# Retention of a two-layer diffusion trunk on one core: two passes over the heads, and latent projections in pairs by seven block products

## The chip, the cores and the metric

The kernel runs on one core of a Trainium2 chip. The metric is the device time of one execution in microseconds (us); a kernel's time is the median over its runs. The engines are PE (matmul), DVE (vector), ACT (scalar), POOL (GpSimd) and SP, which here only issues loads and stores.

## The reference, cut to what matters

The trunk has two layers over 512 latent tokens and 256 context tokens of width 1024; each layer has a mixer and a gated feed-forward part (FFN), with RMS norms, shift, scale and gate around each. The mixer of layer 1 is a bidirectional retention of 8 heads (keys 128 wide, values 256). Context tokens give no output there (`ctx_out` is false), only the state from which the latent scans start:

```python
q, k, v, g = jnp.split(h_lat @ w_in, splits, axis=-1)
q = apply_rope(q.reshape(B, T, H, dk), cos, sin)
k = apply_rope(k.reshape(B, T, H, dk) * dk ** -0.5, cos, sin)
kc, vc = jnp.split(h_ctx @ w_in[:, RET_QK_WIDTH:2 * RET_QK_WIDTH + RET_V_WIDTH], [RET_QK_WIDTH], axis=-1)
for d in range(2):
    lg = log_decay[d]
    s_ctx = retention_final_state(rev(kc), rev(vc), lg)
    outs_lat.append(rev(retention_chunked(rev(q), rev(k), rev(v), lg, s_ctx)))
o = outs_lat[0] + outs_lat[1]
on = ((o - mu) * lax.rsqrt(var + EPS)) * gn_g          # per head
y_lat = (jax.nn.silu(g) * on) @ w_out
```

The layer's conditioning (six vectors of 1024 from `silu(c) @ ada_w[i] + ada_b[i]`) is computed in twelve halves of 512.

## The kernel before, in words

Every fp32 operand of a matmul is split into two parts, hi and lo (`split`, L97): ACT copies it rounded (hi), DVE subtracts (lo). A product (`mm3`, L140) is three matmuls: hi by hi, hi by lo, lo by hi. A unit of weights (`unit`, L101) is 128x1024 numbers that SP's queue loads into a ring of three raw buffers and `split` turns into one of a few slots (`at_slot`, L124; `slot`, L128).

The retention (L1146 to L1488) comes after FFN 0. Its inputs stand in SBUF, turned and split: `hl`, the latent tokens (512 columns), and `hc`, the context tokens (256), built from the residual stream by `build_h` behind the finisher (L641) of FFN 0; `need(chunk)` (L470) builds what isn't built yet. One loop runs over the heads (L1385). Head 0 is special, as its tokens come only then. Each other head does in turn:

- k and then q of all latent tokens (`proj_t`, PSUM names `rk`, `rq`), 24 matmuls of 512 columns each, with the rotation on ACT, DVE and POOL (`rope`, L1192: `m1`, `sw`) and between them the transposes `rt` of the head before (`gated`, L1358), whose gated and normed output goes to two features `gt`
- the output product of head h-1 (`out_group`, L626) for h up to 5, added into y in SBUF by DVE (`yr<-wr,yr`)
- the transposes of k (`k_nat`, L1217), values for the context and the latent tokens (`nat`, L1269: PSUM name `rn`, 48 matmuls of 256 columns for two tiles of 128 tokens), scores (`score`: `rs`, `sd`), states of context and latent chunks (`states`, L1241: `stc`, `stl`), then the gates by `nat` again
- inside and across the chunks (`within`, `across`: `ro`, `rx`, sums in `of`), the context keys of the next head (`k_ctx`, L1203: `rkc`), and the norm (`norm`, L1330: `rbs`, `rmv`, `rrr`, `on`).

The outputs of heads 5 to 7 are summed at the end in PSUM (`part`, L1461), added to y and handed to the finisher. Beside all this, `bg` (L244) steps background jobs: six halves of conditioning (L1886) by `ada_half` (L257), which multiplies on DVE, eight operations 512 wide in each half (`acc<-ar,cs,acc`), and folds them with `ac` or `ag` matmuls. The hybrid layer's halves go another way (`ada_packed`, L333): eight matmuls `ad` with the weights as they come.

The order of work is the order in which the program is written: each engine takes its instructions in that order, and POOL's and SP's queues of transfers likewise. Buffers come free by the rings and slots of the pools.

The FFNs already multiply blocks. The right operand is cut into 2 x 2 blocks (`alloc_blocks` L501, `build_piece` L523), seven sums and single blocks of it are kept (`block_sums`, L559), seven of the weights are made for each piece, and seven products replace eight; their results meet in PSUM (several products onto one sum) or in SBUF. There POOL adds pieces of y to DRAM by accumulating transfers (`yd<-yp`).

Of the kernel before, what the change touches and what calls it, by code (L numbers as in the profile page):

```python
# [31 lines left out]
GF = 2  # L32
ND = 389
EARLY = 2
MLP_PIECES = (
    ((0, (4, 5), 0, False), (0, (0,), 256, True), (1, (1, 2), 0, False), (1, (3,), 256, True)),
    ((0, (0, 1), 0, True), (1, (2,), 0, False), (1, (3,), 128, True)),
)
# [30 lines left out]
class Trunk:  # L69
# [430 lines left out]

    def alloc_blocks(self, l):  # L501
# [8 lines left out]
    def staged(self, l, half, k, w):  # L510
# [3 lines left out]
        if self.sb is None:  # L514
            homes = ((self.bp, "y0"), (self.lp, "y4"), (self.lp, "y5"), (self.lp, "G1")), ((self.bp, "y0"), (self.bp, "y1"))
# [7 lines left out]
    def build_piece(self, l, half, toks, c0, last, xn, ab):  # L523
# [20 lines left out]
        if half:  # L544
# [5 lines left out]
        for m in range(4):  # L550
            src = self.staged(l, half, 2 * m, 2)
            if half and m < 2:
                self.split(self.b12[0][m], self.b12[1][m], src)
            else:
                b = self.blk[(11, 21)[m // 2] if not half else 22]
                ks = slice(2 * (m % 2), 2 * (m % 2) + 2)
                self.split(b[:, 0, ks, :], b[:, 1, ks, :], src)

    def block_sums(self, l):  # L559
# [17 lines left out]
        hb = self.bp.tile([P, 6144], F32R, name=f"hs{l}", tag="h1", bufs=1)  # L577
        for i, x in enumerate((2, 4)):
            self.blk["t", x] = hb[:, 8 * n * i : 8 * n * (i + 1)].rearrange("p (x k c) -> p x k c", x=2, k=4)
        self.rest = hb[:, 16 * n :]  # L580
# [60 lines left out]
    def finisher(self, gates, src, ab, name, xts, last=False, mlp=None):  # L641
# [4 lines left out]
        def fin(t, y, sums=None):  # L646
            if not done and not last:
                if mlp is None:
                    self.alloc_h(name)
                else:  # L650
# [10 lines left out]
            if not last:  # L661
                for b in self.pend:
                    b[0] -= 1
                if mlp is None:
                    for c, pair in ((2, (4, 5)), (0, (0, 1)), (1, (2, 3))):
                        if t == pair[1]:
                            self.pend.append([1, c, lambda c=c: self.build_h(c, done, ab, name)])
                else:
                    for half, toks, c0, end in MLP_PIECES[mlp]:
                        if t == toks[-1]:  # L670
                            go = lambda h=half, ts=toks, c0=c0, e=end: self.build_piece(mlp, h, ts, c0, e, done, ab)
                            self.pend.append([1, half, go])
# [473 lines left out]
    def retention(self, y, final):  # L1146
        S, V, T, G, a = self.S, self.V, self.T, self.G, self.a
        KS = float(np.float32(P) ** np.float32(-0.5))
        with ExitStack() as ctx:
            rp = self.phase(ctx, "retp", 3)  # L1150
            dist = rp.tile([P, 2 * ND], F16, name="dist", tag="dist")
            self.load(dist, a["dist"])
            cos = rp.tile([P, 512], F32, name="cos", tag="cos")
            self.load(cos, a["cos"])
            sin = rp.tile([P, 512], F32, name="sin", tag="sin")
            self.load(sin, a["sin"])
            dec = rp.tile([P, 16], F32, name="dec", tag="dec")
            self.load(dec, a["decay"].broadcast_to([P, 16]))
            gng = rp.tile([P, 16], F32, name="gng", tag="gng")
            self.load(gng, a["gn_col"])  # L1160
            w8 = lambda w: [x.rearrange("p (k c) -> p k c", k=4) for x in w]

            def home(name):
# [842 lines left out]
```

## Time and profile before

| what | value |
| --- | --- |
| median of 3 runs | 1862.83 us (1862.36 to 1866.6) |
| the profiled execution's own time | 1862.51 us |
| its span in the trace | 1860.7 us |
| PE busy | 96% |
| DVE, ACT, POOL busy | 71%, 54%, 17% |
| mean granted TensorE clock | 0.987 |

The profile is of one execution, and its span lies 1.8 us under that execution's own time. All operations are recorded by one helper and so carry one line number (L61, in the changed kernel L64); rows are told apart by the names of their tiles, with the buffer numbers left out. In a row, `x` is a count, `out<-in` the tiles, and a bracket the idle time ahead of the operation and what ended it. The context keys' first matmuls, `rkc`, come at 933.8 us, and those of the following heads at 992.8, 1063.4, 1130.5, 1196, 1262, 1328 and 1387; the first of them marks the retention's begin, the others the last part of the head before. The tail runs from 1452 to 1500, and FFN 1 begins inside it, about 1481.

### The profile page before, as it was taken

The numbers are of one execution on the slowest core, as the hardware profiler recorded it, in microseconds if no ns is written. First come the engines' busy times: TensorE is split into PE (matmuls) and PEld (weight loads), VectorE is DVE, ScalarE is ACT, GpSimd is POOL, SyncE is SP. The second block draws the span as 40 slices with busy tenths as digits, with TensorE's granted clock in tenths as the row PEclk, the third lists the DMA queues.
The fourth block names the chain that finished last, engine by engine and source line by source line (L and its number), as shares of the span: only waits on it lengthen the run. The fifth ranks groups of instructions, "written<-read, shape, count | busy, mean of one in ns | idle before, by whom it ended". The sixth has DMA issues, their size and how long they took to land. (4 is left out here: it accounts for less than half of the span.)

```text
span 1860.7 us, 28942 instructions
## 1 busy us (share of the span) xinstructions
PE 1783.2 (96%) x11104; PEld 1587.4 (85%) x11104; DVE 1319.3 (71%) x2235; ACT 1005.4 (54%) x1815; POOL 314.5 (17%) x451
## 2 busy tenths in 40 slices
PE   7999999999999999998999999999999899999998
PEld 4887777889989899998787988998999689889887
DVE  4543567579787787778876676666555798888887
ACT  4534567456565555555564433443444476666664
POOL 1111211100223222221121011001000201122221
PEclk9999999999999999999999999999999989999999
DMA  8433332324587777776642431332222335777772
GB/s 308 136 105 106 105 103 74 120 82 147 154 198 159 164 159 155 170 148 153 222 151 63 130 109 52 126 114 66 83 69 62 120 108 150 185 182 175 185 172 103
DMA packets 83627, 249.79 MB, mean 134 GB/s; under 512 B 10912, under 2 KB 12448, under 8 KB 83488
## 3 DMA queue, kind: packets, MB, share of 16 engines
q1 hardware_dynamic: 56960, 199.00, 32.7%
q0 software_dynamic: 25952, 48.83, 15.3%
q8 instruction: 87, 1.43, 0.3%
q14 instruction: 52, 0.43, 0.1%
q10 hardware_dynamic: 576, 0.11, 0.0%
HBM read 191.28 MB, written 39.85 MB: 124 GB/s over the span
## 5 line engine op out<-in xcount | busy, mean ns | idle before, releaser
L61 DVE SCALAR_TENSOR_TENSOR cv<-pre,cw,cv 128x769 f32<-128x769 f32 (+1 forms) x176 | 152.9, 881 | 6.5 <-ACT cv L61 5.9
L61 DVE SCALAR_TENSOR_TENSOR acc<-ar,cs,acc 128x512 f32<-128x512 f32 x160 | 118.2, 751 | 30.0 <-DMA ar<-in_adaw 19.0
L61 ACT ACTIVATE cv<-pre,cw 128x770 f32<-128x770 f32 (+1 forms) x88 | 81.0, 922 | 43.1 <-DVE pre L61 41.8
L61 POOL DMA_DIRECT2D yf<-yp x64 | 55.7, 871 | 264.9 <-ACT yp L61 229.2
L61 POOL DMA_DIRECT2D yd<-yp x54 | 46.1, 861 | 190.8 <-ACT yp L61 186.9
L61 ACT COPY yp<-wf 128x512 f32<-128x512 f32 x118 | 67.8, 576 | 17.4 <-PE wf L61 17.3
L61 ACT ACTIVATE pre<-px 128x256 f32<-128x256 f32 (+2 forms) x160 | 54.1, 365 | 39.2 <-PE px L61 38.8
L61 POOL DMA_DIRECT2D yd<-ypg x54 | 44.8, 852 | 153.9 <-ACT ypg L61 153.2
L61 POOL TENSOR_SCALAR rrr<-rmv 128x2 f32<-128x2 f32 x16 | 3.1, 194 | 349.7 <-DVE rmv L61 349.7
L61 ACT ACTIVATE g<-cv 128x770 fp32r<-128x770 f32 (+1 forms) x44 | 32.5, 738 | 34.5 <-DVE cv L61 34.2
L61 PE MATMUL px<-hs,wd 128*128 128x384 f32 x240 | 45.4, 337 | 0.4 <-DVE pre L61 0.4
L61 PEld LDWEIGHTS px<-hs,wd 128*128 128x128 f32 x240 | 42.3, 188 | 2.3 <-DVE pre L61 0.8
L61 ACT ACTIVATE cv<-cv 128x770 f32<-128x770 f32 (+1 forms) x44 | 32.7, 744 | 17.2 <-DVE cv L61 17.1
L61 DVE TENSOR_TENSOR g<-cv,g 128x770 fp32r<-128x770 f32 (+1 forms) x44 | 36.2, 822 | 6.7 <-ACT g L61 6.2
L61 ACT ACTIVATE pre<-py 128x384 f32<-128x384 f32 (+1 forms) x40 | 17.3, 434 | 41.8 <-DVE cv L61 24.4
L61 PEld LDWEIGHTS px<-hs 128*128 128x128 f32 x240 | 30.8, 190 | 10.2 <-DVE pre L61 9.1
L61 PE MATMUL px<-hs 128*128 128x256 f32 x240 | 32.5, 285 | 7.0 <-DVE pre L61 7.0
L61 DVE TENSOR_TENSOR pre<-pre,pz 128x256 f32<-128x256 f32 (+1 forms) x60 | 20.9, 371 | 23.5 <-PE pz L61 23.4
L61 DVE TENSOR_TENSOR cv<-cv 128x770 f32<-128x770 f32 (+1 forms) x44 | 36.2, 822 | 1.0
L61 POOL TENSOR_TENSOR tm<-slab,mask 128x256 f32<-128x256 f32 (+1 forms) x32 | 25.6, 832 | 65.7 <-DVE sst L61 65.5
L61 ACT ACTIVATE sc<-sc,sst 128x512 f32<-128x512 f32 x32 | 23.2, 726 | 23.9 <-DVE sc L61 21.6
L61 ACT COPY ypg<-wf 128x512 f32<-128x512 f32 x54 | 30.8, 577 | 8.0 <-PE wf L61 7.9
(2535 smaller groups left out, 6751.2 us busy)
## 6 DMA issues: line engine op xcount, KB each, us to landing
ar<-in_adaw SPq DMA_DIRECT2D x96, 512.0 KB, 4.2
yf<-yp POOLq DMA_DIRECT2D x64, 256.0 KB, 4.4
yd<-yp POOLq DMA_DIRECT2D x54, 256.0 KB, 5.2
yd<-ypg POOLq DMA_DIRECT2D x54, 256.0 KB, 4.7
fin<-xd SPq DMA_DIRECT2D x10, 512.0 KB, 5.6
xd<-xd SPq DMA_DIRECT2D x8, 512.0 KB, 2.6
xn<-in_x SPq DMA_DIRECT2D x6, 512.0 KB, 5.7
xb<-in_x SPq DMA_DIRECT2D x6, 512.0 KB, 3.9
```

The costliest lines, as they stand in the source:

```text
L61: r = f(*p, **k)
```

## The change

The retention takes its heads in two passes. The first does only the context: keys, values and the final states of all eight heads. The raw states go to DRAM (`rsd`). During it the latent tokens, which now are cut into blocks of 256 tokens by 512 features (`alloc_ret`, `build_piece`), are built, and their sums are made behind context heads 1 to 4 (`block_sums("r")`).

The second pass does the latent heads. k and q of a head are one pair: their weights are the two rows of a 2 x 2 block matrix, and `kq_product` makes them by seven products of 12 matmuls, 256 columns each, into three PSUM tiles X, Y, Z. Values and gates are the other pair (`vg_product`: seven products of 24 matmuls). The weights' sums are made in place in the raw buffers by `sums`: per pair three additions on POOL (`rwk`, `rwq` 512 wide, `rwa`, `rwb` 1024) and one on DVE, with seven splits for a value pair and six for a key pair. These run as generators that are stepped between the products (`in_kq`, `in_vg`). The context's state is loaded back (`cs`) and split.

The output of heads 0 to 4 is cut into eight pieces a head, woven between the products of the next one (`out_steps`, `o`): ACT copies the piece into one of two buffers (`ryp`), and a transfer on POOL's queue adds it to DRAM (`yr`); y is loaded at the end. Head h-1's pieces start behind the sixth product of head h's k and q. The norm writes in place (`of`), `gated` reads `g`. The six conditioning halves beside it go by `ada_packed`. The loads of the decay numbers and a part of `dist` move ahead of FFN 0, those of `cos`, `sin` and `gng` to the sixth context head.

```diff
+CTX_BG = 1
...
+    def alloc_ret(self):
+
+        self.bn = 256
+        self.hb = [self.bp.tile([P, 3, 2048], F32R, name=f"h{i}c", tag=f"h{i}", bufs=1) for i in range(2)]
+        self.hc = [x[:, 0].rearrange("p (k c) -> p k c", k=KD) for x in self.hb]
+        view = lambda i, r: self.hb[i][:, r].rearrange("p (x k c) -> p x k c", x=2, k=4)
+        self.blk = {11: view(0, 1), 21: view(0, 2), 22: view(1, 1), ("t", 2): view(1, 2)}
+        self.sa = self.bp.tile([P, KD, 256], F32, name="sar", tag="sa", bufs=1)
+        self.sb = None
...
+        if l == "r":
+            hb = self.bp.tile([P, 3, 1024], F32R, name="sar4", tag="sa", bufs=1)
+            self.blk["t", 4] = hb[:, 0:2].rearrange("p x (k c) -> p x k c", k=4)
+            self.rest = hb[:, 2]
...
+                            self.pend.append([9 if mlp == "r" else 1, half, go])
...
+            states_d = [self.dp.tile([P, 512], F32, name=f"rsd{h}", tag=f"rsd{h}") for h in range(8)]
+            yd = [self.dp.tile([P, D], F32, name=f"yr{t}", tag=f"yr{t}") for t in range(4)]
...
+            def ctx_states(h):
+                d = hd[h]
+                kd = d["kdc"]
+                pc = self.ps(f"stc{h}", "A", (P, 2, 256))
+                for i in range(2):
+                    for t in range(2):
+                        self.mm3(pc[:, i], [x[:, t, i] for x in kd], [x[:, t] for x in d["vc"]], t == 0, t == 1)
+                sc = self.t2k(f"sc{h}")
+                S.copy(sc, pc.rearrange("p i v -> p (i v)"))
+                self.load(states_d[h], sc)
...
+            def sums(a1, a2, b1, b2, put, both=None):
+
+                add = lambda o, x, y: G.tensor_tensor(out=o, in0=x, in1=y, op=ALU.add)
+                if both:
+                    put("a1", both)
+                else:
+                    put("a1", a1)
+                    yield
+                    put("a2", a2)
+                add(a1, a1, b1)
+                add(b1, b1, b2)
+                yield
+                put("s2", b1)
+                V.tensor_tensor(out=b1, in0=a1, in1=b2, op=ALU.add)
+                add(a2, a2, b1)
+                yield
+                put("q3", b1)
+                yield
+                put("q4", a2)
+                yield
+                put("s3", a1)
+                yield
+                put("b2", b2)
...
+            def prod_t(ps, w, b, kind):
+                for k in range(4):
+                    c = slice(k * P, (k + 1) * P)
+                    self.mm3(
+                        ps,
+                        [x[:, c] for x in w],
+                        [self.blk[b][:, x, k, :] for x in range(2)],
+                        k == 0 and kind != "onto",
+                        k == 3,
+                        kind == "onto",
...
+            def kq_product(h, after):
+
+                d = hd[h]
+                w = d["kq"]
+                pre = [rp.tile([P, 512], F32, name=f"{x}p{h}", tag=f"pre{i}") for i, x in enumerate("kq")]
+                X, Y = (self.ps(f"{x}kq{h}", "A", (P, 256)) for x in "XY")
+                Z = self.ps(f"Zkq{h}", "C", (P, 256))
+                C = [slice(0, 256), slice(256, 512)]
+                k = d["k"] = [kq_[:, 0, x] for x in range(2)]
+                q = d["q"] = [kq_[:, 1, x] for x in range(2)]
+                prod_t(X, w["a1"], 11, "only")
+                S.copy(pre[0][:, C[0]], X)
+                after(0)
+                prod_t(Z, w["a2"], 21, "only")
...
+                V.tensor_tensor(out=pre[0][:, C[0]], in0=pre[0][:, C[0]], in1=Z, op=ALU.add)
+                after(1)
+                prod_t(Y, w["s2"], ("t", 1), "only")
+                S.activation(pre[1][:, C[1]], Y, AF.Copy, scale=-1.0)
+                after(2)
+                prod_t(X, w["q3"], ("t", 2), "onto")
+                S.copy(pre[0][:, C[1]], X)
+                after(3)
+                prod_t(Y, w["q4"], 22, "onto")
+                V.tensor_tensor(out=pre[0][:, C[1]], in0=pre[0][:, C[1]], in1=Y, op=ALU.add)
+                after(4)
+                d["kl"] = pre[0]
+                one, two = rope(pre[0], k, KS, f"k{h}")
+                one()
+                prod_t(X, w["s3"], ("t", 3), "onto")
+                V.tensor_tensor(out=pre[1][:, C[1]], in0=pre[1][:, C[1]], in1=X, op=ALU.subtract)
+                after(5)
+                two()
+                prod_t(X, w["b2"], ("t", 4), "onto")
+                S.activation(pre[1][:, C[0]], X, AF.Copy, scale=-1.0)
+                one, d["q_two"] = rope(pre[1], q, 1.0, f"q{h}")
+                one()
+                after(6)
...
+            def vg_product(h, after, o):
+
+                d = hd[h]
+                w = d["vg"]
+                v = d["v"] = [rp.tile([P, 4, 256], F32R, name=f"rv{i}{h}", tag=f"rv{i}", bufs=1) for i in range(2)]
+                g = d["g"] = rp.tile([P, 4, 256], F32, name=f"rg{h}", tag="rg", bufs=1)
+                X, Y, Z = (self.ps(f"{x}vg{h}", "A", (P, 2, 256)) for x in "XYZ")
+                C = [slice(0, 2), slice(2, 4)]
+                prod_n(X, w["a1"], 11, "only")
+                d["q_two"]()
+                pre = rp.tile([P, 2, 256], F32, name=f"vp0{h}", tag="pre1", bufs=1)
+                S.copy(pre, X)
+                after(0)
+                k_nat(h)
+                prod_n(Z, w["a2"], 21, "only", o)
+                V.tensor_tensor(out=pre, in0=pre, in1=Z, op=ALU.add)
+                self.split(v[0][:, C[0]], v[1][:, C[0]], pre)
+                after(1)
...
+            def context(h):
+                d = hd[h]
+                d["sc"] = rp.tile([P, 2, 256], F32, name=f"cs{h}", tag="cs", bufs=1)
+                self.load(d["sc"].rearrange("p i v -> p (i v)"), states_d[h])
+                d["st"] = [rp.tile([P, 4, 256], F32R, name=f"st{i}{h}", tag=f"st{i}", bufs=1) for i in range(2)]
+                self.split(d["st"][0][:, 0:4:3], d["st"][1][:, 0:4:3], d["sc"])
...
+            def out_steps(h, feats, wo):
+                if not parts:
+                    t = rp.tile([P, 2, 512], F32, name="ryp", tag="yp")
+                    parts.extend(t[:, i] for i in range(2))
+
+                def piece(t, n):
+                    c, o = self.gcol(t), H[n]
+                    ps = self.ps(f"w{h}{t}{n}", "B")
+                    for f, (g, w) in enumerate(zip(feats, wo)):
+                        self.mm3(ps, [x[:, c] for x in g], [x[:, o] for x in w], f == 0, f == 1)
+                    parts.append(parts.pop(0))
+                    S.copy(parts[-1], ps)
+                    if h == 0:
+                        G.dma_start(yd[t][:, o], parts[-1])
+                    else:
+                        G.dma_start(yd[t][:, o], parts[-1], accum_op=ALU.add)
+
+                return [lambda t=t, n=n: piece(t, n) for t in range(4) for n in range(2)]
...
+            blocks = self.block_sums("r")
+            ctx_weights(0)
+            self.need(2)
+            kq = vg = None
+            for h in range(8):
+                ctx_keys(h)
+                if h == 1:
+                    self.need(1)
+                if h:
+                    ctx_states(h - 1)
+                ctx_values(h)
+                if h < 7:
+                    ctx_weights(h + 1)
+                else:
+                    kq = kq_weights(0)
+                    next(kq)
+                    next(kq)
+                if h == 0:
+                    self.need(0)
+                elif h < 5:
+                    next(blocks, None)
+                if h == 5:
+                    self.load(cos, a["cos"])
+                    self.load(sin, a["sin"])
+                    self.load(gng, a["gn_col"])
+                if h == 6:
+                    vg = vg_weights(0)
+                self.bg(CTX_BG)
...
+                def in_kq(n):
+                    if n == 0:
+                        o()
+                        if h in (0, 6, 7):
+                            step(vg)
+                    elif n == 1:
+                        o()
+                        if 0 < h < 6:
+                            wo.append(w_out(h - 1))
+                    elif n == 2:
...
+                    elif n == 5:
+                        if h:
+                            f.extend(gated(h - 1))
+                            if h < 6:
+                                out.extend(out_steps(h - 1, f, list(wo)))
+                            else:
+                                feats.extend(f)
...
+                def in_vg(n):
+                    nonlocal later
+                    if n == 0:
+                        step(vg)
+                        self.bg()
+                    elif n == 1:
+                        step(vg)
+                    elif n == 2:
+                        step(vg)
+                        context(h)
+                        self.bg()
+                        if h < 7:
+                            later = kq_weights(h + 1)
+                    elif n == 3:
+                        step(vg)
+                        score(h, 0)
+                    elif n == 4:
+                        self.bg()
+                    elif n == 5:
+                        score(h, 1)
+                        states(h)
+                        within(h, 0)
+                        step(later)
...
+                kq_product(h, in_kq)
+                vg_product(h, in_vg, o)
...
+                        self.load(y[t], yd[t])
...
-        self.jobs = [self.ada_half(1, h, 1, g3 if h < 6 else None) for h in range(4, 10)]
+        self.jobs = [self.ada_packed(1, h, 1, g3 if h < 6 else None) for h in range(4, 10)]
```

Where latent head 3 begins, POOL's order before has the last part of head 2's norm (`rrr`), head 3's decay matrix (`e`), the sine products of k and q, and the clearing and first row of a conditioning half:

```order
L61 TENSOR_SCALAR rrr2_10872<-rmv2_10871 128x2
L61 TENSOR_TENSOR rrr2_10872<-rrr2_10872,mhalf_102 128x2
L61 TENSOR_TENSOR e03_10947<-e03_10947,e13_10949 128x384
L61 TENSOR_TENSOR e03_10947<-e03_10947,ident_80 128x128
L61 TENSOR_TENSOR swk3_10932<-swk3_10932,sin_8821 128x512
L61 TENSOR_TENSOR swq3_10996<-swq3_10996,sin_8821 128x512
L61 MEMSET acc170_11019 128x512
L61 DMA acc170_11019<-in_adab_row 1x16x32
```

The same place of the changed kernel, between heads 3 and 4 (`yr` are the pieces of y in DRAM, `rwa` and `rwb` the raw weights of values and gates):

```order
L64 TENSOR_TENSOR e04_12528<-e04_12528,e14_12530 128x384
L64 TENSOR_TENSOR rrr3_12426<-rrr3_12426,mhalf_102 128x2
L64 TENSOR_TENSOR e04_12528<-e04_12528,ident_80 128x128
L64 DMA yr2_8799<-ryp_10688 128x512
L64 DMA yr3_8800<-ryp_10688 128x512 x2
L64 TENSOR_TENSOR rwa14r_12387<-rwa14r_12387,rwb14r_12391 128x1024
L64 TENSOR_TENSOR rwb14r_12391<-rwb14r_12391,rwb24r_12389 128x1024
L64 TENSOR_TENSOR swk4_12579<-swk4_12579,sin_8786 128x512
L64 TENSOR_TENSOR swq4_12629<-swq4_12629,sin_8786 128x512
L64 TENSOR_TENSOR rwa24r_12393<-rwa24r_12393,rwb14r_12391 128x1024
```

The pieces' transfers and two wide additions now stand ahead of the sine products on POOL, and a third one behind them; the clearing of `acc` is gone.

DVE's order before, from the rotation of head 3's k to that of its q (`gt` are head 2's features, `yr` here y in SBUF):

```order
L61 SCALAR_TENSOR_TENSOR m1k3_10931<-rk3_10904,cos_8819 128x512
L61 SCALAR_TENSOR_TENSOR gt12_10954<-rt20_10955,gng_8825,gt02_10953 128x512
L61 TENSOR_TENSOR m1k3_10931<-m1k3_10931,swk3_10932 128x512
L61 SCALAR_TENSOR_TENSOR gt12_10954<-rt21_10962,gng_8825,gt02_10953 128x512
L61 TENSOR_TENSOR rk13_10930<-m1k3_10931,rk03_10929 128x512
L61 SCALAR_TENSOR_TENSOR m1q3_10995<-rq3_10946,cos_8819 128x512
L61 TENSOR_TENSOR yr00_9661<-wr200_11038,yr00_9661 128x512
L61 TENSOR_TENSOR m1q3_10995<-m1q3_10995,swq3_10996 128x512
```

And now (`kp` and `qp` are k and q before the rotation, which meet the sums X, Y, Z; `rwo` and `rvg` are lo parts of split weights):

```order
L64 TENSOR_TENSOR kp3_11809<-kp3_11809,Zkq3_11813 128x256
L64 TENSOR_TENSOR rwo21l_11859<-rwo21r_11860,rwo21h_11858 128x1024
L64 TENSOR_TENSOR rvga13l_11915<-rwa13r_11745,rvga13h_11914 128x1024
L64 TENSOR_TENSOR kp3_11809<-kp3_11809,Ykq3_11812 128x256
L64 TENSOR_TENSOR rvga23l_11932<-rwa23r_11751,rvga23h_11931 128x1024
L64 TENSOR_TENSOR qp3_11810<-qp3_11810,Xkq3_11811 128x256
L64 SCALAR_TENSOR_TENSOR kp3_11809<-kp3_11809,cos_8785 128x512
L64 SCALAR_TENSOR_TENSOR gt12_11956<-rt20_11957,gng_8784,gt02_11955 128x512
L64 SCALAR_TENSOR_TENSOR gt12_11956<-rt21_11964,gng_8784,gt02_11955 128x512
L64 TENSOR_TENSOR kp3_11809<-kp3_11809,swk3_11937 128x512
L64 TENSOR_TENSOR rvgs23l_11993<-rwb13r_11749,rvgs23h_11992 128x1024
```

The additions into y are gone from DVE, and the meets of the products and four wide splits stand between the steps of the rotation.

More of the change, by code (lines that the diff above doesn't have):

```diff
@@ L543, in build_piece @@
             return
-        if half:
+        if half and l != "r":
             n = self.bn
@@ new lines, in prod_t, with prod_n @@
+            def prod_t(ps, w, b, kind):
+                for k in range(4):
+                    c = slice(k * P, (k + 1) * P)
+                    self.mm3(
+                        ps,
[4 more added lines that the diff above has]
+                        kind == "onto",
+                    )
+            def prod_n(ps, w, b, kind, between=lambda: None):
+                for i in range(2):
+                    if i:
+                        between()
+                    for k in range(4):
+                        c = slice(i * P, (i + 1) * P)
+                        self.mm3(
+                            ps[:, i],
+                            [self.blk[b][:, x, k, c] for x in range(2)],
+                            [x[:, k, :] for x in w],
+                            i == 0 and k == 0 and kind != "onto",
+                            k == 3,
+                            True,
+                        )
@@ new lines, in two @@
+                def two():
+                    V.tensor_tensor(out=x, in0=x, in1=sw, op=ALU.add)
+                    self.split(dst[0], dst[1], x)
+                return one, two
+            def kq_product(h, after):
[34 more added lines that the diff above has]
+                after(6)
@@ L1253, in states @@
+                for i in range(2):
+                    for t in range(2):
+                        vt = 2 * i + t
+                        self.mm3(pl[:, i], [d["kd"][:, x, t, i] for x in range(2)], [x[:, vt] for x in d["v"]], t == 0, t == 1)
                 cm = self.t2k(f"cm{h}", shape=(P, 2, 256))
-                self.split(st[0][:, 0:4:3], st[1][:, 0:4:3], pc)
-                sc = self.t2k(f"sc{h}", shape=(P, 2, 256))
-                S.copy(sc, pc)
                 for n, i in ((0, 1), (1, 0)):
@@ L1463, in part @@
                         for i in fs:
-                            self.mm3(sums[t, n], [x[:, c] for x in feats[i]], [x[:, o] for x in ws[i]], i == 0, i == 5)
-                within(h, 0)
+                            self.mm3(sums_[t, n], [x[:, c] for x in feats[i]], [x[:, o] for x in ws[i]], i == 0, i == 5)
+                step(later)
+                step(later)
+                within(h, 1)
+                step(later)
+                step(later)
+                step(later)
+                if h < 7:
+                    vg = vg_weights(h + 1)
+                if h < 5:
+                    wo[:] = []
+                    wo.append(w_out(h))
                 across(h, 0)
                 across(h, 1)
-                if h < 7:
-                    k_ctx(h + 1, wk)
-                within(h, 1)
                 across(h, 2)
```

415 lines of the change are left out of this document (233 added, 182 removed).

## The prediction

> **What bounds the kernel now.** I read the page first, then the busy times by stretches, the waits of PE, the timeline of PE at one boundary of two heads, and the groups by shape inside one head. The page:
>
> ```profile
> span 1860.7 us, 28942 instructions
> PE 1783.2 (96%) x11104; PEld 1587.4 (85%) x11104; DVE 1319.3 (71%) x2235; ACT 1005.4 (54%) x1815; POOL 314.5 (17%) x451
> ```
>
> PE is busy nearly all the time, so the question is whether that holds in the stage that the change rewrites. By stretches (head 0, heads 2 and 3, the tail of the retention, the start of the second FFN; columns as in the first row):
>
> ```profile
> core 0: us, PE busy (x) PEld busy (x) DVE busy (x) ACT busy (x) POOL busy (x), PEclk, DMA share, GB/s
> 934.00:993.00 59.00, 54.38 (x444) 52.63 (x443) 42.80 (x65) 36.10 (x64) 9.34 (x12) 1.00 0.44 139
> 1063.40:1130.50 67.10, 65.89 (x449) 59.90 (x449) 43.91 (x76) 26.86 (x38) 7.50 (x11) 1.00 0.32 99
> 1130.50:1196.00 65.50, 65.31 (x451) 59.27 (x450) 43.31 (x75) 26.78 (x39) 6.94 (x10) 1.00 0.30 96
> 1452.00:1500.00 48.00, 37.26 (x190) 31.13 (x189) 35.74 (x59) 29.45 (x65) 10.07 (x18) 0.89 0.31 107
> 1500.00:1560.00 60.00, 59.62 (x450) 56.40 (x450) 57.43 (x91) 44.08 (x79) 0.93 (x1) 1.00 0.34 110
> ```
>
> A head costs 65.5 us and PE works 65.3 of them, with DVE at 43.3. So a matmul less is time less, as long as PE stays fed. The last row shows how far that goes: in the FFN, which already multiplies by blocks, DVE is busy 57.43 of 60 us and PE still 59.62, with hardly any work on POOL. What PE waits for between 934 and 1452:
>
> ```profile
> PE rt L61 <- DVE rg L61: 2.4, 2, 1.4
> PE htc L61 <- DVE hc L61: 2.4, 3, 1.3
> PE wr L61 <- DVE yr L61: 1.0, 1, 1.0
> ```
>
> These are few microseconds in 518, so there is little to gain but the work itself. Now the price of a matmul, from start to start, since their recorded spans overlap:
>
> ```profile
> 995.80 1.58 PE L61 MATMUL ro<-rv,sd 128*128 128x256 f32 x12
> 997.21 1.55 PE L61 MATMUL rx<-st,rq 128*128 128x512 f32 x6
> 998.60 0.39 PE L61 MATMUL rk<-h0c,rwk1h 128*128 128x512 f32 x1
> ...
> 1004.19 0.38 PE L61 MATMUL rt<-ident,rg 128*128 128x128 f32 x2
> 1005.92 0.33 PE L61 MATMUL rt<-ident,rg 128*128 128x128 f32 x1 [1.35 <-DVE rg L61]
> 1007.35 0.77 PE L61 MATMUL rt<-ident,rg 128*128 128x128 f32 x5 [1.09 <-DVE rg L61]
> ...
> 1008.84 0.63 PE L61 MATMUL rq<-h0c,rwq1h 128*128 128x512 f32 x1
> 1009.27 0.63 PE L61 MATMUL rq<-h1c,rwq1h 128*128 128x512 f32 x1
> ```
>
> Twelve of 256 columns take 997.21 - 995.80 = 1.41, so 0.1175 us each. The 24 of `rk`, 512 columns wide, take 1004.19 - 998.60 = 5.59, so 0.233 each. Halving the width costs nothing: 2 x 0.1175 is 0.235. After the two idle times at `rt` the next matmuls are 0.43 apart: the clock was halved for about eight of them, 1.6 us more.
>
> **The change: PE's work.** By the counts of the two orders, k and q had 336 matmuls of 512 and 96 of 256 columns, 78.3 + 11.3 = 89.6 us; now 672 of 256, 79.0 us: -10.6. The latent values and gates had 1536 of 256 and have 1344: -192 x 0.1175 = -22.6. The context's 192 + 384 matmuls, scores, states and outputs keep their number. Together **-33.2 us**.
>
> The six conditioning halves beside the retention go from DVE to PE, 48 matmuls more. The stage before shows their price:
>
> ```profile
> 182.35 1.92 PE L61 MATMUL ad<-ar,c 128*32 128x512 f32 x8
> 184.20 0.39 PE L61 MATMUL s<-ka,q 128*128 128x256 f32 x1
> ```
>
> Eight in 1.85 us, so 48 x 0.231 = +11.1; the eight `ac` products go (-8 x 0.232 = -1.9), and wider transposes and the two gate products give back about 1: **+10 us**. What DVE did for them, 48 x 0.745 = 36 us, is free beside PE and goes.
>
> **Waits that go.** The latent blocks are now built behind the first two context heads, 72 matmuls of 0.1175 each, 8.5 us of cover where `htc` waited 2.4 us. `wr` no longer waits for DVE's additions into y (1.0). The wait at `rt` after head 0 (2.4 + 1.6) goes as it stands, but is priced anew below. In sum 7.4: **-7.4 us**.
>
> **DVE's work.** The price of each kind, in head 3 (all groups are 128 partitions high):
>
> ```profile
> L61 DVE TENSOR_TENSOR yr<-wr,yr 128x512 f32<-128x512 f32 x8 | 5.5, 689 | 1.1 <-PE wr L61 1.0
> L61 DVE SCALAR_TENSOR_TENSOR acc<-ar,cs,acc 128x512 f32<-128x512 f32 x8 | 6.0, 745 | 0.1
> L61 DVE SCALAR_TENSOR_TENSOR of<-rx,e,of 128x256 f32<-128x256 f32 x8 | 3.6, 476 | 1.2 <-PE rx L61 1.2
> L61 DVE TENSOR_SCALAR on<-of,rmv,rrr 128x256 f32<-128x256 f32 x4 | 2.4, 630 | 1.1 <-POOL rrr L61 1.1
> L61 DVE BATCH_NORM_STATS2 rbs<-of 128x6 f32<-128x256 f32 x4 | 1.7, 423 | 0.0
> L61 DVE TENSOR_TENSOR sd<-rs,e 128x256 f32<-128x256 f32 x4 | 1.5, 413 | 0.0
> L61 DVE TENSOR_TENSOR rwg31l<-rwg31r,rwg31h 128x1024 fp32r<-128x1024 f32 x1 | 1.2, 1226 | 0.5 <-ACT rwg31h L61 0.5
> L61 ACT ACTIVATE rwg31h<-rwg31r 128x1024 fp32r<-128x1024 f32 x1 | 1.1, 1067 | 1.2 <-DMA rwg31r<-in_ret_vg 1.2
> L61 POOL TENSOR_TENSOR swq<-swq,sin 128x512 f32<-128x512 f32 x1 | 1.3, 1302 | 5.7 <-ACT swq L61 5.7
> L61 POOL TENSOR_TENSOR e<-e,ident 128x128 f32<-128x128 f32 x1 | 0.5, 460 | 0.1
> ```
>
> A latent head of the new kernel has on DVE: 11 operations 1024 wide (7 splits for v and g, one for k, two for the output rows, one sum), 13.5 us; 21 of 512 (5 splits and a sum for k and q, 6 for the rotation, 5 for v and g, 4 for scores and states), 14.5; two `gt` at about 0.75, 1.5; ten like `of` and `cm`, 4.8; 11 plain ones of 256, 4.6; the norm's 4 `on`, `rbs` and `rmv`, 4.9; four `kd` of 128 columns, 1.5 (at most 4 x 0.48, `of`'s price at 256). Sum 45.3 us. PE's head: 252 matmuls of the seven products, 29.6; scores, states and `ro` 48 x 0.1175 = 5.6; `rx` 2.8; transposes 1.3: 39.3; plus, where eight pieces of an earlier head's output are woven in, 48 x 0.233 = 11.2: 50.5. The pieces of head h-1 start in the second half of head h. So head 0 and head 7 have none, heads 1 and 6 have four, and heads 2 to 5 have eight. Taken alone, DVE at 45.3 fits under 50.5, but not under head 0's 39.3 plus two conditioning pairs (41.2), from which DVE has 42 to do (no `gt`, one output row less).
>
> POOL is new in this. It adds blocks of weights, three of 512 columns at 1.30 and three of 1024 (from the rows of 128 and 512 columns 2.2 ns a column, so 2.4; twice the 512 gives 2.6; I take 2.5) in each head: 11.4 us. And POOL and DVE hinder each other, as these rows show:
>
> ```profile
> 135.24 0.40 POOL L61 TENSOR_SCALAR slab<-slab 128x256 f32<-128x256 f32 x1 [4.76 <-DMA slab<-in_rpb]
> ...
> 192.29 2.76 POOL L61 TENSOR_SCALAR slab<-slab 128x256 f32<-128x256 f32 x1 [3.50 <-DMA slab<-in_rpb]
> 192.43 1.22 DVE L61 TENSOR_TENSOR wk2l<-wk2r,wk2h 128x1024 fp32r<-128x1024 f32 x1
> 193.57 1.22 DVE L61 TENSOR_TENSOR wv2l<-wv2r,wv2h 128x1024 fp32r<-128x1024 f32 x1
> ...
> 1140.10 1.00 POOL L61 TENSOR_TENSOR e<-e,e 128x384 f32<-128x384 f32 x1
> 1140.17 1.62 DVE L61 TENSOR_SCALAR on<-of,rmv,rrr 128x256 f32<-128x256 f32 x2 [1.09 <-POOL rrr L61]
> ```
>
> The same POOL operation takes 0.40 alone and 2.76 when two splits of weights run back to back on DVE: it ended only after both. The other way, two `on` beside a POOL product took 1.62. I take half of POOL's 11.4 as lost to DVE (bounds: none, all): 45.3 + 5.7 = 51.0 a head. Against PE that gives: head 0, 47.7 to 41.2, +6.5; head 1, 51.0 to 44.9 + 1.9 + the rest of its conditioning, about 48, +3; heads 2 to 5, level, 1 us each for the order of things, +4; head 6, 48.5 (no output rows) to 44.9, +3.5; the boundary from 6 to 7, +3: PE has rx, six products and `rt` in 12 us, DVE across, norm, two splits and three meets 15. **+20 us**, all as waits of PE for DVE at `rt` and at the last product onto X.
>
> **What I cost at nothing.** ACT gains 40 splits of 1024 at 1.07, 40 of 512 and 32 more copies, about 115 us over the stage; it was busy 26.8 of 65.5 and stays near two thirds. The loads grow by 24 units and the y additions; 40 additions of 256 KB go by POOL's queue, which then issues each only once ACT has copied the piece, and behind it on that queue stand the norm's `rrr` and `swk`. On SP's queue each state's store waits for its copy, and the next head's weights stand behind it; they are needed a head later, 11 us. For that and for the start I take **+3 us** (bounds 0 and 16, two us a context head).
>
> **The sum.** -33.2 + 10 - 7.4 + 20 + 3 = -7.6. Against the profiled execution, 1862.5 us (span 1860.7), which is within 0.4 of the median of the three runs (1862.83): 1855. Its own range is 1847 to 1863 (stalls 12 to 28).
>
> The pieces of y in the first FFN, which go the way that the retention's pieces now go (two groups, and the landing of the transfer):
>
> ```profile
> L61 POOL DMA_DIRECT2D yd<-yp x54 | 46.1, 861 | 190.8 <-ACT yp L61 186.9
> L61 ACT COPY yp<-wf 128x512 f32<-128x512 f32 x118 | 67.8, 576 | 17.4 <-PE wf L61 17.3
> ...
> yd<-yp POOLq DMA_DIRECT2D x54, 256.0 KB, 5.2
> ```
>
> **The rivals.** (1) PE stays fed as in the FFN's row, where DVE at 57.43 of 60 cost it 0.4 us: the stalls are 6 instead of 20 and the start 2, so -22.6 and **1840**. For it speaks that DVE's work was laid between the products; against it that FFN has no sums on POOL. Chance 0.25. (2) Slower: POOL's sums and DVE's splits exclude each other throughout. Then a head has 45.3 + 11.4 = 56.7 us of work for the two: head 0 +12, head 1 +9, heads 2 to 5 +5 each, head 6 +9, boundary +3, in sum 53, and -33.2 + 10 - 7.4 + 53 + 3 = +25.4: **1888**. The point from which it decides is 28 us of stalls, where about 0.62 of POOL's time falls on DVE. Chance 0.17. The Trainium skill, "SBUF — State Buffer", section "SBUF: two separate sides", says that DVE and GpSimd share one pair of ports, locked for a whole instruction, and that a DVE operation with two SBUF inputs takes it against a GpSimd operation that reads SBUF; some two thirds of DVE's 45.3 us are such operations, which by the rule gives stalls of about 31 and 1866. The 2.76 us row agrees with it for POOL as the one that waits; that a split waits for POOL no row shows. (3) The y pieces (rows ahead of this part): two buffers only, one piece per 2.8 us while k and q run, against a round trip that the same pieces of the first FFN show: copy 0.58, issue 0.86, landing 5.2. That is 6.6, 1 us over the 5.6 of two pieces, so ACT is held about 2 us in each of five heads: +10, **1865**. Chance 0.10. (4) The context pass waits for its weights, +2 us a head, 16 in place of 3: **1868**. Chance 0.06. The first forecast keeps 0.42.
>
> **How the numbers follow.** What a measurement can tell from no change is 0.3%, 5.6 us. Faster by more (under 1857.2): all of rival 1 and 0.31 of the first case, 0.56. Within: 0.11 of it, rival 3 and a little of 4, 0.22. Slower: rival 2 and most of 4, 0.22. The range that leaves out a tenth on each side reaches from rival 1 to the middle of rival 2: 1839 to 1875.
>
> **What would show it.** In the new profile a context head should take 10 to 11 us of PE, a latent head 2 to 5 about 51, and heads 0 and 6 should show the waits of PE for DVE (`Xkq`, `rt`). POOL's `rwa` and `rwb` sums should take 2.5 us alone and over 3 beside splits. If PE in the heads is busy over 98%, rival 1 holds. If heads 2 to 5 take over 55 us, rival 2 does. If ACT waits for `ryp`, it is rival 3.

## The result, and the profile after

The changed kernel takes 1886.86 us (median of four, 1878.99 to 1894.07), the kernel before beside it 1864.55: ratio 1.0119, 95% interval 1.0076 to 1.0162, so it is slower by about 1.2%. The forecast was 1855, its range ended at 1875. The page of the profiled execution, the slowest of the four:

```profile
span 1892.3 us, 29833 instructions
PE 1785.2 (94%) x11240; PEld 1587.8 (84%) x11240; DVE 1424.1 (75%) x2349; ACT 1114.6 (59%) x2038; POOL 454.3 (24%) x533
```

DVE gained 105 us and POOL 140, PE hardly any. By stretches (the whole context pass, then latent heads 0, 1, 3 and 6; columns as before):

```profile
937.00:1044.50 107.50, 98.12 (x746) 87.27 (x745) 75.21 (x117) 72.05 (x146) 13.97 (x18) 0.97 0.68 219
1044.50:1095.90 51.40, 46.51 (x345) 43.01 (x345) 35.83 (x46) 28.16 (x45) 20.50 (x11) 0.93 0.34 117
1095.90:1150.00 54.10, 51.70 (x369) 47.18 (x368) 43.94 (x77) 31.55 (x51) 17.47 (x17) 0.94 0.44 142
1207.40:1265.30 57.90, 54.70 (x394) 49.31 (x392) 47.70 (x76) 35.90 (x57) 26.73 (x23) 1.00 0.58 150
1378.40:1426.60 48.20, 46.09 (x349) 43.92 (x348) 43.15 (x72) 31.13 (x50) 21.31 (x18) 1.00 0.36 83
```

A middle head takes 57.9 us, and no engine is busy all of it: PE 54.7, DVE 47.7. I took the starts of all matmuls and counted each up to its price (0.234 for 512 columns, 0.119 for 256 and fewer). From the first `rkc` to the first transposes for FFN 1 that gives, before, 512.2 us of work and 21.2 lost; after, 489.0 and 74.8. So by this count the work fell by 23.2, and the loss grew by 53.6: in the context pass 21.1 is lost, in heads 0 to 6 10.5, 7.8, 5.4, 5.8, 6.0, 5.8 and 3.3, from there on 9.2. The count is too low for the conditioning: its `ad` matmuls start two or four at a time (a few ns apart), and such a group then takes 0.43 or 0.52 us. Their 96 records count 7.5 us in it and take about 15. Put right, the work fell by about 15.6 and the loss grew by about 46; the context pass lost 17.5, heads 0 to 3 one us less each than stated, the others as stated.

What PE waits for in the latent heads:

```profile
PE Xkq L64 <- DVE qp L64: 10.4, 5, 2.4
PE kn L64 <- DVE kp L64: 4.2, 3, 1.4
PE stl L64 <- DVE rv L64: 4.0, 5, 1.1
PE stl L64 <- ACT rv L64: 2.3, 1, 2.3
```

The costliest is the last product onto X of k and q, behind the transposes. Before it, DVE has to take the sum that stands in X into q (`qp<-qp,Xkq`); I call such an operation a meet. In head 3, PE, then DVE, then POOL at that place:

```profile
1221.55 1.04 PE L64 MATMUL rt<-ident,rg 128*128 128x128 f32 x8
1224.85 1.70 PE L64 MATMUL Xkq<-sar 128*128 128x256 f32 x12 [2.26 <-DVE qp L64]
```

```profile
1220.43 0.41 DVE L64 TENSOR_TENSOR kp<-kp,Ykq 128x256 f32<-128x256 f32 x1
1220.81 3.65 DVE L64 TENSOR_TENSOR rvga23l<-rwa23r,rvga23h 128x1024 fp32r<-128x1024 f32 x1
1224.38 0.41 DVE L64 TENSOR_TENSOR qp<-qp,Xkq 128x256 f32<-128x256 f32 x1
1224.71 2.54 DVE L64 SCALAR_TENSOR_TENSOR kp<-kp,cos 128x512 f32<-128x512 f32 x1
1227.18 1.40 DVE L64 SCALAR_TENSOR_TENSOR gt<-rt,gng,gt 128x512 fp32r<-128x512 f32 x2
```

```profile
1220.68 2.69 POOL L64 TENSOR_TENSOR rwa13r<-rwa13r,rwb13r 128x1024 f32<-128x1024 f32 x1
1223.45 3.27 POOL L64 TENSOR_TENSOR rwb13r<-rwb13r,rwb23r 128x1024 f32<-128x1024 f32 x1
1226.67 1.75 POOL L64 TENSOR_TENSOR swk<-swk,sin 128x512 f32<-128x512 f32 x1
```

DVE's split of the second value unit should take 1.22 us. POOL's addition began 0.13 us before it; the split ended 1.09 after that addition did. Only then can DVE do the 0.41 us for which PE has been waiting. I call such a wait of DVE for a POOL instruction a hold. The next operation, `kp<-kp,cos`, is stretched from 0.69 to 2.54 by the second addition. `gt`, which reads PSUM, runs beside POOL's `swk` unstretched. In the context pass PE waits for loads of the conditioning:

```profile
968.33 0.28 PE L64 MATMUL stc<-vch,kdc 128*128 128x256 f32 x1
971.31 1.92 PE L64 MATMUL ad<-ar,c 128*32 128x512 f32 x4 [2.70 <-DMA ar<-in_adaw]
975.67 0.41 PE L64 MATMUL rvc<-rcv20h,h0c 128*128 128x256 f32 x1
975.88 0.41 PE L64 MATMUL rvc<-rcv20l,h0c 128*128 128x256 f32 x1
```

Behind the 2.70 us the matmuls start 0.21 apart, not 0.1175, for about 6 us, so the wait costs twice. The granted clock of this stretch (the third number from the end) agrees:

```profile
965.50:983.50 18.00, 15.30 (x96) 11.90 (x95) 13.47 (x22) 10.50 (x22) 3.11 (x4) 0.81 0.68 209
```

### The profile page after: what moved, and what is told of

It reads as the page before. It is cut to its first block, busy times and chain, and to the rows that moved or that the text cites. A ratio compares the mean times of both kernels' runs of the same rounds, so it can differ in the third digit from the quotient of the medians.

```text
span 1892.3 us, 29833 instructions
## 1 busy us (share of the span) xinstructions
PE 1785.2 (94%) x11240; PEld 1587.8 (84%) x11240; DVE 1424.1 (75%) x2349; ACT 1114.6 (59%) x2038; POOL 454.3 (24%) x533
## 5 line engine op out<-in xcount | busy, mean ns | idle before, releaser
L64 DVE SCALAR_TENSOR_TENSOR acc<-ar,cs,acc 128x512 f32<-128x512 f32 x112 | 81.7, 746 | 27.0 <-DMA ar<-in_adaw 16.1
L64 POOL DMA_DIRECT2D yr<-ryp x40 | 32.9, 822 | 58.2 <-ACT ryp L64 50.8
L64 PE MATMUL ad<-ar,c 128*32 128x512 f32 (+1 forms) x320 | 41.5, 530 | 4.6 <-DMA ar<-in_adaw 4.5
L64 PE MATMUL px<-hs,wd 128*128 128x384 f32 x240 | 45.3, 336 | 0.4 <-DVE pre L64 0.4
L64 ACT COPY ryp<-w 128x512 f32<-128x512 f32 x40 | 23.4, 584 | 27.1 <-DMA yr<-ryp 14.9
L64 DVE CUSTOM_DVE_ANT_0 sc<-s,tm 128x256 f32<-128x256 f32 x32 | 13.5, 421 | 33.5 <-PE s L64 24.6
L64 DVE TENSOR_TENSOR pre<-pre,pz 128x256 f32<-128x256 f32 (+1 forms) x60 | 20.9, 371 | 23.2 <-PE pz L64 23.1
L64 ACT ACTIVATE sc<-sc,sst 128x512 f32<-128x512 f32 x32 | 23.2, 726 | 25.3 <-DVE sc L64 23.0
```

Source lines behind the costliest of these rows:

```text
L64: r = f(*p, **k)
```

## The experiments

The first explanation (P, place): POOL's additions cost because one holds up a DVE operation ahead of a meet. Its rivals: T, DVE's and POOL's times add up to a head's pace (the prediction's rival 2), and C, POOL is not the cause. Times are medians, each ratio against the kernel before on the same chip. The chips differ from run to run; on them the kernel before took 1864.0 to 1866.4.

**The changed kernel again.** No edit. 

> The changed kernel once more, beside the kernel before on the same chip, as the base for the three others. All theories: 1880 to 1894 us, ratio about 1.012, and in the trace a middle head (2 to 5) of 56 to 58 us with 5 to 6 us in which PE gets less than its matmuls' price. If the spread of its times comes from the context pass, the context pass differs between the two traces by more than the latent heads do.

Measured: 1886.05, ratio 1.0100 (1.0078 to 1.0123). Its trace has 106.2 us of context pass against 107.5, heads 0 and 1 take 49.3 and 52.4, where they took 51.4 and 54.1, and the middle ones agree within 0.4. Of the 6.4 us between the two spans heads 0 and 1 make 3.8 and the context pass 1.3.

**POOL's additions left out.**

```diff
-                add(a1, a1, b1)
-                add(b1, b1, b2)
...
-                add(a2, a2, b1)
```

> POOL's six additions of weights in each head are left out (the sums are then not those of the seven products); everything else stays, DVE's one addition and all splits too. Theory P (place): an addition on POOL holds up the one DVE operation that stands ahead of the meet for which PE waits, so PE loses about 2.4 us a head at the transposes and 1.2 at the latent states: without the additions about 5 of the 5 to 6 us lost in heads 2 to 5 fall to 2, in all heads together 25 to 30 us, time about 1858. Theory T (throughput, the rival of the prediction): DVE's 45.3 and POOL's 11.4 us exclude each other and 56.7 us is what a head takes: without them PE sets the pace at 52 to 53, 4 to 5 us less in each of heads 2 to 5 and more in 0, 1 and 6, about 30 us, 1857. Theory C (POOL is not the cause: the order of DVE's and ACT's splits alone, or the pieces of y): under 8 us less, above 1877.

Measured: 1857.28, ratio 0.9943 (0.9921 to 0.9966): 29 us less. C falls. Head 3 there, by stretches and on DVE:

```profile
1187.90:1241.80 53.90, 53.90 (x393) 49.15 (x392) 40.26 (x76) 36.25 (x57) 13.95 (x17) 1.00 0.64 162
```

```profile
1201.66 1.22 DVE L64 TENSOR_TENSOR rvga23l<-rwa23r,rvga23h 128x1024 fp32r<-128x1024 f32 x1
1202.79 0.42 DVE L64 TENSOR_TENSOR qp<-qp,Xkq 128x256 f32<-128x256 f32 x1
1203.12 0.69 DVE L64 SCALAR_TENSOR_TENSOR kp<-kp,cos 128x512 f32<-128x512 f32 x1
```

PE is fed without a gap, and the same DVE operations have their own lengths.

**The hold without the sum.** The additions read the lo parts that released them and write an unused tile; the sums are missing. A wide addition is two instructions of 512 columns here.

```diff
-                add(a1, a1, b1)
-                add(b1, b1, b2)
+                def hold(lo):
+                    for c in H[: a1.shape[-1] // 512]:
+                        add(dummy, dummy, lo[:, c])
...
+                hold(lo)
+                hold(lo)
```

> POOL's six additions of weights run at the same moments, released by the same lo parts and with the same columns in all, but they read those lo parts and write a tile that nothing reads; the sums of the weights are left out, and sine reads the cosine's table (for room). So DVE meets POOL as in the changed kernel, but no split and no matmul waits for a sum. If POOL's additions cost by holding DVE while they run (theory H): most of the 29 us that leaving them out saved are back, 1876 to 1888, and the wait for the meet of q at the transposes is 2 us or more again. If they cost by being late themselves (theory L: split and product wait for the sum, as after the reordering that was slower): near the kernel without additions, 1855 to 1865.

Measured: 1882.63, ratio 1.0085 (1.0053 to 1.0117): 25 of the 29 us are back, though nothing waits for a sum. PE's waits there:

```profile
PE stl L64 <- DVE rv L64: 9.3, 6, 3.4
PE Xkq L64 <- DVE qp L64: 8.0, 7, 1.6
```

That the additions hold DVE is shown: in head 3 the split `rvga23l` takes 2.52 us here, though it reads nothing that they write. That their results come late is not the main cost. Two things keep the 25 us from being the price of the holds alone. The wide additions are cut in two, and a cut changes the holds, as the pieces below show. And the additions keep POOL busy, on whose queue the pieces of y go out: ACT waits 14.9 us for their two buffers (`ryp`) in the changed kernel, 15.9 here, 3.1 without the additions. No run separates what PE loses that way. Its waits for ACT behind the context pass are 6.7 of 28.9 us in the changed kernel, 3.6 of 28.9 here and 0.3 of 4.9 without the additions; the others are nearly all for DVE.

**The additions on DVE.**

```diff
-                add = lambda o, x, y: G.tensor_tensor(out=o, in0=x, in1=y, op=ALU.add)
+                add = lambda o, x, y: V.tensor_tensor(out=o, in0=x, in1=y, op=ALU.add)
```

> All four additions of a pair run on DVE, POOL has none. Theory T: DVE has 45.3 + 5.7 = 51 us a head (three additions of 1.21 and three of 0.68), under PE's 52 to 53, and nothing is excluded: about as fast as without additions, 1860. Theory P: two additions of 1.21 us stand on DVE where the hold of 2.4 us stood, ahead of the same meet: the wait at the transposes stays at about 2.4 us, the later ones shrink; 1876 to 1888. Theory C: slower than the changed kernel, since DVE gets more to do, 1890 to 1900.

Measured: 1868.87, ratio 1.0010 (0.9991 to 1.0029), between the two. Its waits:

```profile
PE Xkq L64 <- DVE qp L64: 7.2, 6, 1.9
PE kn L64 <- DVE kp L64: 4.7, 2, 3.1
```

The lengths of DVE's operations in head 3 sum to 52.4 us both here and in the changed kernel; the head takes 55.2 here and 57.9 there, with DVE busy 47.0 and 47.7. The sum alone doesn't set the time, against T.

**Another order, additions on POOL or on DVE.** The order that is built need not be that of the program's text: in the order of DVE shown ahead of the prediction `qp<-qp,Xkq` stands ahead of `kp<-kp,cos`, and `kq_product` writes them the other way round. `fixed` has the written order kept on the engines that it names (V is DVE, G is POOL). First the second value unit and what follows it behind the rotation:

```diff
-                    elif n == 4:
-                        step(vg)
...
                     elif n == 6:
                         step(vg)
+                        step(vg)
...
+                self.fixed = "VG"
                 V.tensor_tensor(out=pre[1][:, C[1]], in0=pre[1][:, C[1]], in1=X, op=ALU.subtract)
```

> The same work in another order: the split of the second value unit and POOL's two wide additions behind it stand behind the rotation of k and q, not ahead of the last meet of q. Theory P: the wait of about 2.4 us at the transposes goes in heads 1 to 6 and k's rotation is no longer stretched, 12 to 20 us less, about 1870; what is new is that the third product of values and gates may wait for its sum, at most 2 us a head. Theory T: the sum of DVE's and POOL's time is the same, so within 5 us of the changed kernel, 1882 to 1892. Theory C: as T.

Measured: 1934.39, ratio 1.0359 (1.0336 to 1.0382). The wait at the meet fell from 10.4 to 2.8, as P said, but others came, and neither P's 1870 nor T's 1882 to 1892 did:

```profile
PE stl L64 <- ACT rv L64: 9.2, 5, 3.5
PE Yvg L64 <- ACT rvgs25h L64: 3.1, 1, 3.1
PE Xkq L64 <- DVE qp L64: 2.8, 4, 1.4
```

The third product of values and gates (`Yvg`), whose weights now come late, waits about 16 us in all, where I had allowed 2 a head.

With the additions on DVE, and only the meet of q moved ahead (`step(vg)` at step 5, kept in order on DVE): 

> All additions on DVE, and of DVE's work the second value unit's split and the additions behind it are kept behind the last meet of q, not ahead of it. Against the additions on DVE alone (1869, 7.2 us of waits for that meet and about 1.5 us of low clock behind each): theory P (place) expects the waits to go and 8 to 12 us less, 1857 to 1861, under the kernel before. Theory T (only the sum of DVE's work counts): within 3 us of 1869.

Measured: 1872.64, ratio 1.0030 (1.0011 to 1.0049), no gain: the wait at the meet fell from 7.2 to 2.0, that of `kn` grew from 4.7 to 6.0, and behind the context pass PE's waits are about 17 us in both. So P alone falls too: here the order moved the wait and didn't remove it.

**The additions in pieces.**

```diff
+                def add(o, x, y):
+                    for i in range(0, o.shape[-1], 256):
+                        c = slice(i, i + 256)
+                        G.tensor_tensor(out=o[:, c], in0=x[:, c], in1=y[:, c], op=ALU.add)
```

> The changed kernel, each of POOL's six additions cut into pieces of 256 columns (two or four instructions), the same columns in all, at the same places of both orders. If the length of one hold is what counts (a DVE operation that meets an addition waits for its end, 2.4 us, and PE with it): a hold is at most about 0.6 us now, the wait for the meet of q falls from 10 us to under 4, and 8 to 16 us of the 29 come back: 1870 to 1878. If the sum of POOL's time counts (each piece takes its share from DVE in turn): 1882 to 1892, and the split of the second value unit still takes over 3 us.

Measured: 1913.01, ratio 1.0251 (1.0224 to 1.0278), 27 us slower still. DVE and POOL at the place:

```profile
1215.44 7.96 DVE L64 TENSOR_TENSOR rvga23l<-rwa23r,rvga23h 128x1024 fp32r<-128x1024 f32 x1 [0.17 <-ACT rvga23h L64]
1223.32 0.41 DVE L64 TENSOR_TENSOR qp<-qp,Xkq 128x256 f32<-128x256 f32 x1
```

```profile
1215.31 3.09 POOL L64 TENSOR_TENSOR rwa13r<-rwa13r,rwb13r 128x256 f32<-128x256 f32 x4
1218.07 3.02 POOL L64 TENSOR_TENSOR rwb13r<-rwb13r,rwb23r 128x256 f32<-128x256 f32 x4
1220.78 1.52 POOL L64 TENSOR_TENSOR swk<-swk,sin 128x512 f32<-128x512 f32 x1
```

The split ends only 1.1 us after all nine POOL instructions in the row, which take 7.0 us. DVE was not let in between them, which none of my theories had.

**No conditioning in the context pass.**

```diff
-CTX_BG = 1
+CTX_BG = 0
```

> The changed kernel with no step of the conditioning between the context heads; the steps go to the latent heads, three a head, and what is left to the last. If the context pass loses time because the conditioning's loads come late among the weights (4 to 5 us of waiting at ad, and as much again at a lower clock behind it): the context pass is 6 to 9 us shorter, and the latent heads pay 0 to 4 us back: 1878 to 1882. If the weights' own loads bound the context pass: within 3 us of the changed kernel.

Measured: 1877.32, ratio 1.0052 (1.0034 to 1.0070), 9 us less. The context pass:

```profile
937.20:1030.80 93.60, 87.28 (x716) 84.97 (x715) 73.47 (x116) 70.07 (x145) 11.56 (x14) 1.00 0.63 201
```

It is 12.6 us shorter than in the second trace, of which the eight steps' own work is a part.

**Both taken away** (no POOL additions, `CTX_BG = 0`): 

> Both suspects out: POOL's six additions of a head are left out (their sums are then wrong) and no conditioning runs in the context pass. If these two explain the miss, their savings add: 1857 less 9 is 1848, 7 us under the forecast of 1855, and the latent heads show 0.5 to 2 us lost each. If a third cause is left in the latent heads, the time stays above 1853, since the conditioning that moves into them finds no room.

Measured: 1849.83, ratio 0.9935 (0.9911 to 0.9959). Against the kernel without additions the medians differ by 7.4 us, the intervals of the ratios overlap; in the traces this stage is 7.8 us shorter. No third cause is needed to get back under the forecast. But the forecast has 23 us of stalls in it; against the sum without them, 1832, some 18 us stay unexplained by these two.

**The conditioning back on DVE** (`ada_half` in place of `ada_packed`; sine reads the cosine's table, for room, so the rotation is another one). 

> The six conditioning halves go back to DVE (eight additions of 0.745 us each, and their splits), the rest is the changed kernel; sine reads the cosine's table, for room. What the change moved to PE is priced by it: the prediction took 10 us of PE's time for 48 matmuls, and 36 us of DVE's as free. If DVE is as loaded as the trace says (52 of 58 us a head, its stretched operations counted), 36 us more over six or seven heads can't hide: 15 to 35 us slower than the changed kernel, 1901 to 1921. If DVE has slack (its waits come from place alone), PE's saving counts: 1878 to 1886.

Measured: 1910.14, ratio 1.0215 (1.0169 to 1.0261), 24 us slower than the changed kernel. Its waits:

```profile
PE Xkq L64 <- DVE qp L64: 10.8, 4, 3.7
PE rt L64 <- DVE rg L64: 7.0, 2, 6.2
PE at L64 <- ACT arow L64: 5.4, 2, 4.3
PE ac L64 <- DVE al L64: 4.5, 2, 3.0
```

The last two are waits for the conditioning's own results, 10 us in all. Whether DVE's load makes these late or their place in the order does, the run doesn't separate.

**The additions by transfers**, from the kernel without conditioning in the context pass:

```diff
+                add = lambda o, x: G.dma_start(o, x, accum_op=ALU.add)
+                add(b1, rows[1])
...
+                add(a1, rows[0])
...
+                add(a2, b1)
```

> As the kernel without conditioning in the context pass, and the six additions of a head are done by accumulating transfers on POOL's queue (two from the weights in DRAM, one from SBUF, per pair), not by POOL's arithmetic; DVE keeps its one. Theory H (POOL's arithmetic holds DVE, and that is the cost): DVE is as free as without the sums, and of the 29 us that they cost some 20 to 27 come back, on top of the 9 of the context pass: 1850 to 1860, faster than the kernel before. If the issue of a transfer (0.87 us on POOL) holds DVE as much as an addition does, or the transfers land too late (4 to 5 us each, one behind the other): 1865 to 1885.

Measured: 1886.49, ratio 1.0098 (1.0077 to 1.0120), 9 us slower than its base. The landings in head 3 and the wait that came:

```profile
rwa13r<-in_ret_vg POOLq DMA_DIRECT2D x1, 512.0 KB, 8.0
rwa23r<-rwb13r POOLq DMA_DIRECT2D x1, 512.0 KB, 6.2
```

```profile
PE Xkq L64 <- ACT kp L64: 7.9, 2, 6.1
```

A chain of 6 to 8 us a sum, in order with the pieces of y, fits sums that come too late; ACT waits 26.5 us for `ryp` here. Whether issuing a transfer also holds DVE was not told apart.

**Two versions of both repairs.** All additions on DVE, `CTX_BG = 0`: 

> All additions on DVE, and no conditioning in the context pass. If the two costs are separate: the 1869 us of the additions on DVE less what the context pass gains alone, 1860 to 1865. If the latent heads, where DVE now has about 51 of 53 us, can't take the conditioning in: 1867 to 1872.

Measured: 1860.30, ratio 0.9964 (0.9950 to 0.9979): the fastest of those that leave nothing out, and faster than the kernel before. With the narrow additions left on POOL:

```diff
+                E = G if both else V
+                add = lambda o, x, y: E.tensor_tensor(out=o, in0=x, in1=y, op=ALU.add)
```

> No conditioning in the context pass; the wide additions (values and gates) on DVE, the narrow ones (k and q) on POOL. Against all additions on DVE with the same context pass (1860): DVE has 2 us less of its own a head and three holds of at most 1.4 us more. If holds cost more than DVE's own time for the same sum: 1862 to 1870. If DVE's load as a whole counts: 1855 to 1860.

Measured: 1866.00, ratio 1.0004 (0.9991 to 1.0018). Three additions of 0.7 us moved from DVE to POOL cost 6 us by the medians, and the intervals don't overlap. So DVE's load as a whole doesn't set the time here either. That the holds are what costs is not shown: of the 4.7 us by which this stage differs in the two traces, 2.0 lie in the context pass.

## Why the prediction was wrong

- **PE's work** was mis-sized: forecast -33.2 and +10, which is -23.2; measured about -15.6. k and q gave -10.0 (89.4 to 79.4) and values and gates -21.2 (225.0 to 203.8), near the forecast's -10.6 and -22.6. Most of the rest is the conditioning: its 48 matmuls are 96 records and take about 15 us, where I had 48 x 0.231 = 11.1.
- **"I take half of POOL's 11.4 as lost to DVE"** was near: in head 3 DVE's operations sum to 52.4 us, 7.2 more than the 45.2 without the additions, where I had 5.7 more. But **45.3 and 51.0** are sums of lengths, and neighbours overlap: in the rows without additions the split ends at 1202.88 and the next operation begins at 1202.79. DVE is busy 40.3 us of head 3 without the additions and 47.7 with them, so it never was level with PE.
- **"heads 2 to 5, level, 1 us each for the order of things"** is the step that failed, and with it the +20. I set DVE's sum against PE's and took the excess, and 1 us where there was none, as PE's wait. In these heads PE lost 5.4 to 6.0, though in head 3 DVE is busy only 47.7 of 57.9 us: PE waits behind single operations, and a hold ahead of a meet reaches it (2.26 us in head 3). Without the additions the same heads lose 0.6 to 2.0; with the additions on DVE, busy as long, 2.5 to 3.5. In head 0, 1 and 2 a slower clock came behind a wait. In all, the stage's loss grew by about 46 us, where -7.4 + 20 + 3 is 15.6.
- **Rival 2** gave 53 us of stalls and 1888, and came; I gave it 0.17. That one operation excludes another is shown, for single pairs of them; "throughout" is not: DVE's operations grew by 7.2 us in head 3, not by 11.4. So 1888 came near by luck: its sum (56.7 a head from two times that add up) fits by its size only, since pieces and another order, with the same columns on POOL, took 1913 and 1934, and 8 us of what was missed are PE's own work. The Trainium skill's rule ("SBUF — State Buffer", "SBUF: two separate sides"), an exclusive lock for a whole instruction, agrees with the 3.65 us split and gave 1866 by my reckoning; the 7.96 us split goes beyond it.
- **"For that and for the start I take +3 us"** failed too: the context pass lost 17.5 us. Its place is rival 4's, but the late loads that PE waited for were the conditioning's (4.5 us, and the clock behind it). The repair is worth 9, and 10.8 us stay lost in the pass without it.
- **"What DVE did for them, 48 x 0.745 = 36 us, is free beside PE and goes"** held before the change, not after: put back, it costs 24 us, though PE then does less, and 10 of these are PE's waits for the conditioning's own results.
- **-7.4** came in the main: the building of the blocks (`htr`) has no wait in the context pass, `w` has 0.3 us; `rt` still has 2.2, from which I had priced it anew.
- **Rival 3** came by its sign, not by its price: ACT waits 14.9 us for the landings that free `ryp`, but PE waits only 0.3 us for `ryp` itself. What reaches PE on other ways is open, as said at the hold. **Rival 1**'s condition, PE fed, is what the kernel without additions shows in head 3. ACT's "about 115 us" is more than its terms add up to, some 85 by the rows; 109 were measured.

## What to carry to other kernels

Before giving POOL arithmetic on SBUF data, look at what DVE runs then: an addition of 2.7 us beside a split cost DVE 2.4 us, and PE 2.3 as a meet stood behind. Do not take the longer of two in-order engines' sums as the time of a stage: here DVE was busy 47.7 us and PE 54.7, and a tenth of the head was lost. A background job whose loads can be late belongs where loads are few: here PE paid for the wait and then for the clock.

## What the hardware did that I had not expected

- Short POOL instructions in a row held a DVE operation for the whole row, 7.96 us in place of 1.22; two long ones let it in between (3.65 us). What decides this the runs don't show.
- DVE operations with one input in PSUM ran unstretched beside POOL (two `gt` in 1.40 us).
- One idle time of 2.7 us was followed by about 6 us at half the matmuls' rate. It is not the length alone: behind waits of 2.3 to 2.5 us at the same place of heads 3 to 5 the rate was halved in the second trace of the changed kernel and hardly in the first.
